# Feed-forward products whose stationary operands take every second column of a block of 256

## The chip, the cores and the metric

One core of one Trainium2 chip runs one program. The metric is the device time of that program in microseconds; the median of 3 runs of the kernel before is 1139.22 us (1137.12 to 1141.24).

## What is computed

The reference passes 256 tokens of width 1024, in float32, through seven stages with a residual stream `x`: a feed-forward (f1), a mixer of attention heads (m1), a feed-forward (f2), a second mixer (ab), a feed-forward (f3), a third mixer (cd), a feed-forward (f4), and a last norm. What matters here is the feed-forward, which has 2816 hidden columns:

```python
def _swiglu(x, w_gate, w_up, w_down):
    return (jax.nn.silu(x @ w_gate) * (x @ w_up)) @ w_down

f = _swiglu(_rmsnorm(x, ffn1_pre_g[l]), ffn1_w_gate[l], ffn1_w_up[l], ffn1_w_down[l])
x = x + 0.5 * _rmsnorm(f, ffn1_post_g[l])
```

## The kernel before

Every large product is made of three matmuls on float32r operands: each operand is split into a high part (a cast) and a low part (what the cast lost), and `mm3` (L502) adds high x high, high x low and low x high into the same accumulator in PSUM. Every matmul instruction of TensorE is two records in the trace: a weight load (LDWEIGHTS, engine PEld) that puts 128 stationary columns into the array, and a MATMUL that streams the moving operand, 256 or 512 columns wide. All these matmuls stand at L510.

Weights come as 512 KB tiles through `Stream` (L49): SyncE issues the DMA into `wraw`, ScalarE casts it to `wh` (L87), VectorE (GpSimd for a few) subtracts to `wl` (L92). There are four `wraw` buffers and six of `wh` and `wl`; a tile is split again as soon as TensorE has given its buffer back.

A feed-forward stage is `ffn` (L584). The hidden columns go in 11 blocks of 256. The first block (`first`, L599) keeps the tokens stationary and streams 256 weight columns, so its result is turned by four transposes, `ft`, at j == 1 (L631). For blocks 1 to 10, `gemm_b` (L512) makes gate and up with the weights stationary and the 256 tokens of `xh` or `xl` moving:

```python
c = slice(j * P, (j + 1) * P)
prods.append(((wh[:, k % 4, c], wl[:, k % 4, c]), (act[0][:, k, :], act[1][:, k, :])))
```

`j` is the half of the block, `k` one of 8 slices of the width, so one call is 2 x 8 x 3 = 48 matmuls into the PSUM tile `gb`, and gate and up of a block are 96. ScalarE takes silu of the gate (L636), VectorE multiplies by up (L637), and `split` (L614) writes `hh` and `hl`, 2 chunks of 128 hidden columns x 256 tokens. One block later, `down` (L566) uses a half of the tokens (128 of the 256 in `hh` or `hl`) as the stationary operand and streams 512 columns of the down weights: 2 chunks x 2 halves x 2 column halves x 3 = 24 matmuls into the tiles `f`. The last call takes four chunks (48 matmuls); in f4 some of those go to tiles `f1c`.

The order of the work is the order of the code (the scheduling is manual). `gemm_b` also serves the mixers ab and cd. Two tables at the top set where some operands start in SBUF, in bytes: `XT_AT` (L29) shifts `xh` and `xl` at each stage, by (16, 32) in f1, (64, 128) in f2, (8, 4) in f3 and (128, 224) in f4; `HH_AT` (L30) shifts `hh` and `hl` by 32, 64, 96 and 160 in f1 to f4. The tiles `wh` and `wl` stay at one place.

Other lines that the prediction names: the transposes `E` (L1310) and the plain float32 products `M` (L1317) run between blocks of f3, `za` and `zx` (L993) in ab; a product of plain float32 operands is two loads and two MATMULs in the trace, where float32r has one of each. L1027 (VectorE) and L969 (ScalarE) write or read with steps of 128 bytes, L1372 and L831 are like them with neighbouring floats.

Of the kernel before, what the change touches and what calls it, by code (L numbers as in the profile page):

```python
# [8 lines left out]
F32 = mybir.dt.float32  # L9
# [3 lines left out]
ALU = mybir.AluOpType  # L13
AX = mybir.AxisListType
P = 128
S = 256
# [170 lines left out]
class Kern:  # L187
# [321 lines left out]
                mid()  # L509
            self.nc.tensor.matmul(out=out, lhsT=l, rhs=r, start=start and i == 0, stop=stop and i == n - 1)  # L510

    def gemm_b(self, K=8, act=None):  # L512

        act = act or (self.xh, self.xl)
        tiles = self.ws.take(K // 4)
        p = self.ps("gb")
        pv = p.rearrange("p (j t) -> p j t", j=2)
        for j in range(2):
            prods = []
            for k in range(K):  # L520
                wh, wl = tiles[k // 4]
                c = slice(j * P, (j + 1) * P)
                prods.append(((wh[:, k % 4, c], wl[:, k % 4, c]), (act[0][:, k, :], act[1][:, k, :])))
            self.mm3(pv[:, j, :], prods, True, True)
            self.pump(1)
        return pv
# [39 lines left out]
    def down(self, accs, chunk, n, act, cut=False):  # L566


        tiles = self.ws.take(n)
        last = chunk + n == 22  # L570
        b2 = [(0, slice(0, 512)), (1, slice(512, D))]
        for h in range(2):
            t = slice(h * P, (h + 1) * P)
            m = n - 2 if last else n
            cs = [b2[0], (2, slice(512, 768)), (3, slice(768, D))] if last and len(accs[h]) > 2 else b2
            for i, (b, c) in [(i, b) for i in range(m) for b in cs] + [(i, b) for b in cs for i in range(m, n)]:
                ah, al = act(chunk + i)
                wh, wl = tiles[i]
                k = chunk + i
                self.mm3(accs[h][b], [((ah[:, t], al[:, t]), (wh[:, 0, c], wl[:, 0, c]))],  # L580
                         k == 0 or b > 1 and i == 0, k == 21 or cut and b == h == 1 and k == 17)


    def ffn(self, gpre, gpost, coef, gnext, hooks=None, cut=False):  # L584
        nc = self.nc
        tt = nc.vector.tensor_tensor
        with self.tc.tile_pool(name="ffn", bufs=3) as fp:
            self.php = fp
            self.nff = getattr(self, "nff", -1) + 1
            fp.tile([P, HH_AT[self.nff] // 4], F32, name="gap", tag="gap", bufs=1)  # L590
            hts = {}
            st = {}
            accs = None

            def act(c):
                hh, hl = hts[c // 2]
                return hh[:, c % 2, :], hl[:, c % 2, :]

            def first(h, mid):  # L599
                if h == 0:  # L600
                    st["w"] = self.ws.take(4)
                p = self.ps(f"fh{h}")
                t = slice(h * P, (h + 1) * P)
                for i in range(2):
                    w = st["w"][2 * i:2 * i + 2]
                    prods = [((self.xh[:, k, t], self.xl[:, k, t]), (w[k // 4][0][:, k % 4, :], w[k // 4][1][:, k % 4, :]))
                             for k in range(8)]
                    self.mm3(p[:, i * S:(i + 1) * S], prods, True, True, True, mid if i else None)
                sg = fp.tile([P, S], F32, name="sgf", tag="sgf", bufs=2)
                nc.scalar.activation(out=sg, in_=p[:, 0:S], func=AF.Silu)  # L610
                tt(out=sg, in0=sg, in1=p[:, S:2 * S], op=ALU.mult)
                st[h] = sg

            def split(t, j):  # L614
                hh = fp.tile([P, 2, S], F32R, name="hh", tag="hh")
                hl = fp.tile([P, 2, S], F32R, name="hl", tag="hl")
                nc.scalar.copy(out=hh, in_=t)  # L617
                tt(out=hl, in0=t, in1=hh.bitcast(F32), op=ALU.subtract)  # L618
                hts[j] = (hh, hl)

            self.enter(gpre, first)
            self.gain(gnext)
            if gpost:
                self.gain(gpost)
            for j in range(1, 11):
                gt = self.gemm_b()
                if j == 1:
                    p = self.ps("ft")
                    for c in range(2):
                        for h in range(2):  # L630
                            nc.tensor.transpose(p[:, c * S + h * P:c * S + (h + 1) * P], st[h][:, c * P:(c + 1) * P],  # L631
                                                self.ident)
                    split(p.rearrange("p (c t) -> p c t", c=2), 0)
                up = self.gemm_b()
                sg = fp.tile([P, 2, S], F32, name="sg", tag="sg", bufs=2)
                nc.scalar.activation(out=sg, in_=gt, func=AF.Silu)  # L636
                tt(out=sg, in0=sg, in1=up, op=ALU.mult)  # L637
                split(sg, j)
                for f in (hooks or {}).get(j, []):
                    f()  # L640
                if accs is None:
                    accs = [self.ps2("f0"), self.ps2("f1")]
                if j < 10:
                    self.down(accs, 2 * (j - 1), 2, act, cut)
            if cut:
                accs[1] += [self.ps("f1c")[:, 0:S] for _ in range(2)]
            self.down(accs, 18, 4, act)
            self.close(accs, gpost, coef)
# [978 lines left out]
def _order():  # L1627

    import numpy as np
    p = np.arange(P)  # L1630
    tau = 4 * (p % 32) + p // 32
    return np.concatenate([tau, P + tau])


def _layout(inputs):

    import numpy as np
    g = {k: np.asarray(v) for k, v in inputs.items()}
    A = {n: g[n] for n in _RAW}
    for n in ("ffn1_w_gate", "ffn1_w_up", "ffn1_w_down", "w_qkv", "w_out", "ffn2_w_gate", "ffn2_w_up", "ffn2_w_down", "x",  # L1640
              "ab_w_in_2", "ab_gate_a_w_2", "ab_gate_x_w_2", "ab_w_out_2", "cd_w_in_2", "cd_glu_w_2", "cd_w_out_2"):
        A[n] = A[n][0]
    rows = []
    for n in GAINS:
        if n.startswith("ffn_norm"):
            rows.append(g["ffn_norm_2"][int(n[-1])])
        else:
            rows.append(g[n].reshape(D))
    A["gains"] = np.stack(rows)
    A["x"] = A["x"][_order()]  # L1650
    sw = lambda a: np.ascontiguousarray(a.reshape(2, 2, 16)[:, ::-1]).reshape(64)
    q, k = g["q_norm_g"][0], g["k_norm_g"][0]
    A["gqk"] = np.stack([q, sw(q), k, sw(k)])
    ch = lambda a: a.reshape(4, P).T
    st = lambda a: a.reshape(16, 2, 64).transpose(1, 2, 0).reshape(P, 16)
    parts = {
        "convw": g["ab_conv_w_2"][0].reshape(4, 4, P).transpose(2, 0, 1).reshape(P, 16),
        "convb": ch(g["ab_conv_b_2"][0]), "ba": ch(g["ab_gate_a_b_2"][0]), "bx": ch(g["ab_gate_x_b_2"][0]),
        "lam": ch(g["ab_lambda_2"][0]), "glub": ch(g["cd_glu_b_2"][0]),
        "lr": st(g["cd_lam_re_2"][0]), "li": st(g["cd_lam_im_2"][0]),  # L1660
        "ldt": st(np.repeat(g["cd_log_dt_2"][0][:, None], 64, 1)),
        "d": np.tile(g["cd_d_2"][0].reshape(16, 32).T, (4, 1)),
    }
    A["smalls"] = np.concatenate([parts[n] for n in SM], 1)
    gb = lambda a: a.reshape(16, 2, 64, 16).transpose(1, 2, 0, 3).reshape(P, 16, 16)
    A["s5b"] = np.stack([gb(g["cd_b_re_2"][0]), gb(g["cd_b_im_2"][0])], 1)
    A["s5c"] = np.stack([gb(g["cd_c_re_2"][0].transpose(0, 2, 1)), gb(g["cd_c_im_2"][0].transpose(0, 2, 1))], 1)
    A.update(_constants())
    return {n: np.ascontiguousarray(a) for n, a in A.items()}
# [20 lines left out]
```

## Time and profile before

| | |
|---|---|
| median of 3 runs | 1139.22 us (1137.12 to 1141.24) |
| the profiled execution | 1139.47 us, its span 1137.7 us |
| granted TensorE clock, mean over the span | 0.989 |
| TensorE matmuls | 1108.9 us busy, 7435 records |
| weight loads | 1003.8 us busy |
| VectorE, ScalarE, GpSimd | 681.6, 547.0, 350.7 us busy |
| data moved | 190.99 MB, mean 168 GB/s |

The span runs from the first to the last instruction of the program. Matmuls are pipelined, and the recorded length of one (280 ns for 256 columns) is longer than the distance to the next; so the pace is read from blocks: time of a block by the number of its matmuls. The chain is the sequence of work that ended last, followed back from the end.

### The profile page before, as it was taken

What the parts mean: (1) busy time and instruction counts of PE and PEld (TensorE: products, weight loads), DVE (VectorE), ACT (ScalarE), POOL (GpSimd) and SP (SyncE); (2) the same over time, 40 slices, a digit from 0 to 9 for tenths busy, and PEclk for the clock granted to TensorE, in tenths of its full rate; (3) what the DMA queues carried; (4) which work ended last, traced back from release to release, by engine and by line L of the source; (5) the groups of instructions that cost most, each with busy time, mean ns of one, the idle gap of its engine ahead of it and who ended that gap; (6) DMA issues with size and microseconds to landing.
All of it is one profiled execution on the core that took longest, in us unless ns stands there. A gap on an engine that the chain in (4) does not pass through costs nothing.

```text
span 1137.7 us, 18727 instructions
## 1 busy us (share of the span) xinstructions
PE 1108.9 (97%) x7435; PEld 1003.8 (88%) x7435; DVE 681.6 (60%) x828; ACT 547.0 (48%) x794; POOL 350.7 (31%) x572
## 2 busy tenths in 40 slices
PE   9999999989999999999989999999999999999997
PEld 7999998767879999997966999999989889999996
DVE  5565545789575554557572666556567656554554
ACT  5456445546555443445664544444352465443442
POOL 1006600764320000004151499999414221000000
PEclk9999999999999999999988999999999999999999
DMA  7765665642057656555621675564644336657651
GB/s 233 253 198 169 189 208 163 208 166 75 20 166 235 186 161 216 185 168 173 211 81 38 185 223 174 160 204 147 191 151 149 130 101 202 204 163 220 183 169 57
DMA packets 134361, 190.99 MB, mean 168 GB/s; under 512 B 6017, under 2 KB 109441, under 8 KB 134274
## 3 DMA queue, kind: packets, MB, share of 16 engines
q1 hardware_dynamic: 133536, 187.72, 52.9%
q0 software_dynamic: 736, 2.08, 0.6%
q8 instruction: 58, 0.95, 0.3%
q14 instruction: 29, 0.24, 0.1%
q10 hardware_dynamic: 2, 0.00, 0.0%
HBM read 188.73 MB, written 1.05 MB: 167 GB/s over the span
## 4 chain that ended last, share of the span: by engine, by line
PE 86%; DVE 5%; POOL 3%; issue 2%; ACT 1%; DMA 1%; SPq 0%; POOLq 0%; DVEq 0%; ACTq 0%
PE gb L510 45%; PE f L510 20%; PE wo L510 4%; PE fh L510 4%; PE gh L510 2%; PE ga L510 1%; PE o L826 1%; PE lg L510 1%; DVE x L393 1%; PE lt L1057 1%; PE pT L806 1%; PE M L1317 1%; PE y L1394 1%; DMA wraw<-in_ffn_w_gate_dram 1%; PE tp L357 1%
## 5 line engine op out<-in xcount | busy, mean ns | idle before, releaser
L92 DVE TENSOR_TENSOR wl<-wraw,wh 128x1024 fp32r<-128x1024 f32 x323 | 398.8, 1258 | 179.6 <-ACT wh L87 177.9
L87 ACT CAST wh<-wraw 128x1024 fp32r<-128x1024 f32 x341 | 349.1, 1049 | 214.2 <-PE gb L510 116.3
L510 PE MATMUL gb<-xh,wl 128*128 128x256 f32 x1472 | 412.7, 280 | 0.0
L510 PE MATMUL gb<-xl,wh 128*128 128x256 f32 x1472 | 412.0, 280 | 0.0
L510 PE MATMUL gb<-xh,wh 128*128 128x256 f32 x1472 | 411.9, 280 | 0.0
L510 PEld LDWEIGHTS gb<-xh,wh 128*128 128x128 f32 x1472 | 277.5, 189 | 1.8
L510 PEld LDWEIGHTS gb<-xl,wh 128*128 128x128 f32 x1472 | 277.3, 188 | 1.7
L510 PEld LDWEIGHTS gb<-xh,wl 128*128 128x128 f32 x1472 | 275.8, 187 | 0.0
L510 PE MATMUL f<-wh,hh 128*128 128x512 f32 x348 | 137.3, 395 | 0.0
L510 PE MATMUL f<-wh,hl 128*128 128x512 f32 x348 | 137.0, 394 | 0.0
L510 PE MATMUL f<-wl,hh 128*128 128x512 f32 x348 | 136.9, 393 | 0.0
L617 ACT CAST hh<-sg 128x512 fp32r<-128x512 f32 x40 | 24.8, 621 | 177.5 <-DVE sg L637 177.5
L637 DVE TENSOR_TENSOR sg<-sg,gb 128x512 f32<-128x512 f32 x40 | 27.5, 687 | 119.9 <-PE gb L510 119.2
L337 POOL TENSOR_TENSOR v<-ss 128x1 f32<-128x1 f32 x22 | 5.9, 269 | 253.8 <-ACT xs L329 185.5
L92 POOL TENSOR_TENSOR wl<-wraw,wh 128x1024 fp32r<-128x1024 f32 x21 | 57.2, 2731 | 85.1 <-ACT wh L87 82.3
L332 POOL TENSOR_SCALAR ss<-ss 128x1 f32<-128x1 f32 x6 | 1.6, 270 | 252.6 <-ACT xs L329 252.6
L510 PEld LDWEIGHTS f<-wh,hl 128*128 128x128 f32 x348 | 65.4, 188 | 15.2
L510 PEld LDWEIGHTS f<-wh,hh 128*128 128x128 f32 x348 | 65.4, 188 | 13.4
L510 PEld LDWEIGHTS f<-wl,hh 128*128 128x128 f32 x348 | 65.4, 188 | 13.3
L618 DVE TENSOR_TENSOR hl<-sg,hh 128x512 fp32r<-128x512 f32 x40 | 28.2, 704 | 27.5 <-ACT hh L617 27.5
L510 PE MATMUL wo<-wl,xh 128*128 128x512 f32 x80 | 31.5, 394 | 1.0 <-POOL wl L92 1.0
L510 PE MATMUL wo<-wh,xh 128*128 128x512 f32 x80 | 32.2, 403 | 0.0
(408 smaller groups left out, 1507.7 us busy)
## 6 DMA issues: line engine op xcount, KB each, us to landing
wraw<-in_ffn_w_gate_dram SPq DMA_DIRECT2D x88, 512.0 KB, 4.1
wraw<-in_ffn_w_up_dram SPq DMA_DIRECT2D x88, 512.0 KB, 5.0
wraw<-in_ffn_w_down_dram SPq DMA_DIRECT2D x88, 512.0 KB, 4.1
wraw<-in_ab_w_in_dram SPq DMA_DIRECT2D x20, 512.0 KB, 4.5
wraw<-in_w_qkv_dram SPq DMA_DIRECT2D x18, 512.0 KB, 3.9
wraw<-in_cd_w_in_dram SPq DMA_DIRECT2D x16, 512.0 KB, 4.8
wraw<-in_w_out_dram SPq DMA_DIRECT2D x8, 512.0 KB, 4.5
wraw<-in_ab_w_out_dram SPq DMA_DIRECT2D x8, 512.0 KB, 3.5
```

What stands on the lines that cost most here:

```text
L87: self.nc.scalar.copy(out=h, in_=r)
L92: eng.tensor_tensor(out=l, in0=r, in1=h.bitcast(F32), op=ALU.subtract)
L357: nc.tensor.transpose(p[:, j * P:(j + 1) * P], src[:, (b + j) * P:(b + j + 1) * P], self.ident)
L393: nc.vector.scalar_tensor_tensor(out=xv[:, c], in0=t[:, c], scalar=r, in1=xv[:, c], op0=ALU.mult, op1=ALU.add)
L510: self.nc.tensor.matmul(out=out, lhsT=l, rhs=r, start=start and i == 0, stop=stop and i == n - 1)
L617: nc.scalar.copy(out=hh, in_=t)
L618: tt(out=hl, in0=t, in1=hh.bitcast(F32), op=ALU.subtract)
L637: tt(out=sg, in0=sg, in1=up, op=ALU.mult)
L806: nc.tensor.transpose(p[:, k * S + h * P:k * S + (h + 1) * P], e[:, h, k * P:(k + 1) * P], self.ident)
L826: nc.tensor.matmul(out=o, lhsT=v, rhs=p, start=i % 2 == 0 and n == 0, stop=i % 2 == 1 and n == 5)
L1057: nc.tensor.matmul(out=p[:, 0:384], lhsT=tri[:, 0, :], rhs=s, start=True, stop=False, skip_group_check=True)
L1317: nc.tensor.matmul(out=pv[:, a, :], lhsT=l, rhs=F[:, a, 0:4, :].rearrange("p s q -> p (s q)"), start=r == 0, stop=r == 1)
```

## The change

`gemm_b` gets a switch `deal`. With it, half `j` of a block takes the columns j, j + 2, j + 4 ... of the 256, instead of 128 neighbouring ones. So that each half still holds the same hidden columns, `_layout` reorders the gate and up weights on the host: in each block of 256, column 2i + j of the new array is column 128 j + i of the old one. The four feed-forward stages call it so; the mixers do not. In the same way `down` takes every second token of `hh` and `hl`, and `split` writes them in that order (`turn`). The first block's result comes out in the dealt order, and its transposes pick every second column. The number, order and sizes of all instructions stay as they were, on every engine; what differs is the step of operands.

```diff
--- before.py
+++ after.py
@@ -509,7 +509,8 @@
                 mid()
             self.nc.tensor.matmul(out=out, lhsT=l, rhs=r, start=start and i == 0, stop=stop and i == n - 1)
 
-    def gemm_b(self, K=8, act=None):
+    def gemm_b(self, K=8, act=None, deal=False):
 
         act = act or (self.xh, self.xl)
         tiles = self.ws.take(K // 4)
@@ -519,7 +520,7 @@
             prods = []
             for k in range(K):
                 wh, wl = tiles[k // 4]
-                c = slice(j * P, (j + 1) * P)
+                c = slice(j, None, 2) if deal else slice(j * P, (j + 1) * P)
                 prods.append(((wh[:, k % 4, c], wl[:, k % 4, c]), (act[0][:, k, :], act[1][:, k, :])))
             self.mm3(pv[:, j, :], prods, True, True)
             self.pump(1)
@@ -570,7 +571,7 @@
         last = chunk + n == 22
         b2 = [(0, slice(0, 512)), (1, slice(512, D))]
         for h in range(2):
-            t = slice(h * P, (h + 1) * P)
+            t = slice(h, None, 2)
             m = n - 2 if last else n
             cs = [b2[0], (2, slice(512, 768)), (3, slice(768, D))] if last and len(accs[h]) > 2 else b2
             for i, (b, c) in [(i, b) for i in range(m) for b in cs] + [(i, b) for b in cs for i in range(m, n)]:
@@ -614,8 +615,11 @@
             def split(t, j):
                 hh = fp.tile([P, 2, S], F32R, name="hh", tag="hh")
                 hl = fp.tile([P, 2, S], F32R, name="hl", tag="hl")
-                nc.scalar.copy(out=hh, in_=t)
-                tt(out=hl, in0=t, in1=hh.bitcast(F32), op=ALU.subtract)
+                turn = lambda ap_: ap_.rearrange("p c (t h) -> p c h t", h=2)
+                t = t.rearrange("p c (h t) -> p c h t", h=2)
+                nc.scalar.copy(out=turn(hh), in_=t)
+                tt(out=turn(hl), in0=t, in1=turn(hh).bitcast(F32), op=ALU.subtract)
                 hts[j] = (hh, hl)
 
             self.enter(gpre, first)
@@ -623,15 +627,14 @@
             if gpost:
                 self.gain(gpost)
             for j in range(1, 11):
-                gt = self.gemm_b()
+                gt = self.gemm_b(deal=True)
                 if j == 1:
                     p = self.ps("ft")
                     for c in range(2):
                         for h in range(2):
-                            nc.tensor.transpose(p[:, c * S + h * P:c * S + (h + 1) * P], st[h][:, c * P:(c + 1) * P],
-                                                self.ident)
+                            nc.tensor.transpose(p[:, c * S + h * P:c * S + (h + 1) * P], st[h][:, c::2], self.ident)
                     split(p.rearrange("p (c t) -> p c t", c=2), 0)
-                up = self.gemm_b()
+                up = self.gemm_b(deal=True)
                 sg = fp.tile([P, 2, S], F32, name="sg", tag="sg", bufs=2)
                 nc.scalar.activation(out=sg, in_=gt, func=AF.Silu)
                 tt(out=sg, in0=sg, in1=up, op=ALU.mult)
@@ -1640,6 +1643,10 @@
     for n in ("ffn1_w_gate", "ffn1_w_up", "ffn1_w_down", "w_qkv", "w_out", "ffn2_w_gate", "ffn2_w_up", "ffn2_w_down", "x",
               "ab_w_in_2", "ab_gate_a_w_2", "ab_gate_x_w_2", "ab_w_out_2", "cd_w_in_2", "cd_glu_w_2", "cd_w_out_2"):
         A[n] = A[n][0]
+    deal = lambda a: a.reshape(a.shape[:-1] + (11, 2, P)).swapaxes(-1, -2).reshape(a.shape)
+    for n in ("ffn1_w_gate", "ffn1_w_up", "ffn2_w_gate", "ffn2_w_up", "ffn_w_gate_2", "ffn_w_up_2"):
+        A[n] = deal(A[n])
     rows = []
     for n in GAINS:
         if n.startswith("ffn_norm"):
```

## Rows read from the trace of the kernel before

**Rows 1.** The page, share of the span by engine, then its chain by line.
```profile
PE 1108.9 (97%) x7435; PEld 1003.8 (88%) x7435; DVE 681.6 (60%) x828; ACT 547.0 (48%) x794; POOL 350.7 (31%) x572
...
PE gb L510 45%; PE f L510 20%; PE wo L510 4%; PE fh L510 4%; PE gh L510 2%; PE ga L510 1%; PE o L826 1%; PE lg L510 1%; DVE x L393 1%; PE lt L1057 1%; PE pT L806 1%; PE M L1317 1%; PE y L1394 1%; DMA wraw<-in_ffn_w_gate_dram 1%; PE tp L357 1%
```

**Rows 2.** The chain in order of time: start us, us, what; f1, f2, f4.
```profile
42.80 11.31 PE gb L510 x96
...
54.11 5.45 PE f L510 x24
...
358.60 11.31 PE gb L510 x96
...
369.91 5.60 PE f L510 x24
...
973.23 11.31 PE gb L510 x96
...
984.54 5.57 PE f L510 x24
```

**Rows 3.** Groups by line and shape: busy us, mean ns, idle before.
```profile
L510 PE MATMUL gb<-xh,wl 128*128 128x256 f32 x1472 | 412.7, 280 | 0.0
L510 PEld LDWEIGHTS gb<-xh,wl 128*128 128x128 f32 x1472 | 275.8, 187 | 0.0
...
L510 PE MATMUL f<-wh,hh 128*128 128x512 f32 x348 | 137.3, 395 | 0.0
...
L87 ACT CAST wh<-wraw 128x1024 fp32r<-128x1024 f32 x341 | 349.1, 1049 | 214.2 <-PE gb L510 116.3 <-ACT wh L87 25.2 <-DMA wraw<-in_ffn_w_gate_dram 22.7
L618 DVE TENSOR_TENSOR hl<-sg,hh 128x512 fp32r<-128x512 f32 x40 | 28.2, 704 | 27.5 <-ACT hh L617 27.5
```

**Rows 4.** Windows: stretch, sum, busy of PE PEld DVE ACT POOL, clock, DMA, GB/s.
```profile
42.80:54.11 11.31, 11.31 (x98) 11.31 (x97) 4.71 (x4) 3.65 (x4) 0.00 (x0) 1.00 0.83 266
54.11:59.56 5.45, 5.45 (x26) 4.50 (x26) 3.46 (x15) 4.59 (x6) 0.00 (x0) 1.00 0.05 18
668.40:679.72 11.32, 11.32 (x97) 11.32 (x97) 4.95 (x4) 3.64 (x4) 10.75 (x25) 1.00 0.85 263
679.72:685.32 5.60, 5.60 (x27) 4.49 (x26) 4.21 (x5) 3.57 (x4) 5.50 (x11) 1.00 0.14 27
```

**Rows 5.** Timeline of PE in f3: products with plain f32 operands.
```profile
696.49 1.04 PE L1310 MATMUL E<-ident,bst 128*128 128x128 f32 x8
697.36 0.39 PE L1317 MATMUL M<-Fre,b 128*128 128x128 f32 x2
697.58 0.39 PE L1317 MATMUL M<-Fim,b 128*128 128x128 f32 x2
...
698.92 0.39 PE L1317 MATMUL M<-Fim,b 128*128 128x128 f32 x2
```

**Rows 6.** Timeline of PE in ab: plain f32 products of 256 columns.
```profile
560.18 0.59 PE L993 MATMUL zx<-xc,gw 128*128 128x256 f32 x2
...
562.77 0.59 PE L993 MATMUL zx<-xc,gw 128*128 128x256 f32 x2
```

**Rows 7.** Timeline of DVE, ACT, PE at the end of f1.
```profile
189.67 0.69 DVE L618 TENSOR_TENSOR hl<-sg,hh 128x512 fp32r<-128x512 f32 x1 [0.69 <-ACT hh L617]
...
189.02 0.62 ACT L617 CAST hh<-sg 128x512 fp32r<-128x512 f32 x1 [4.97 <-DVE sg L637]
...
188.03 0.40 PE L510 MATMUL f<-wh,hh 128*128 128x512 f32 x1
```

**Rows 8.** Instructions of L1027 (128-byte steps) and, by groups, of L1372, L969, L831.
```profile
L1027 DVE TENSOR_TENSOR yrg<-tl,ga x4: 586/596/2560, 583.3 to 587.8; 128x256 f32<-128x256 f32 x4
...
L1372 DVE TENSOR_TENSOR st<-st,st 128x256 f32<-128x256 f32 x4 | 1.7, 431 | 0.1
...
L969 ACT COPY xr<-gb 128x256 f32<-128x256 f32 x4 | 1.3, 377 | 1.9 <-PE gb L510 1.9
...
L831 ACT CAST xh<-o 128x256 fp32r<-128x256 f32 x4 | 1.4, 362 | 2.4 <-PE o L826 2.2
```

## Prediction

> **What bounds the kernel now.** First the page [rows 1]: TensorE is busy for 97% of the span, and the chain that ended last is 45% `gb` (gate and up products) and 20% `f` (down products). Second the chain in order of time [rows 2]: a block of two gate and up products is 96 `gb` matmuls in 11.31 us, 117.8 ns each, and the same in f1, f2 and f4; a down block is 24 `f` matmuls, 5.45 us in f1 (227.1 ns each), 5.60 in f2 (233.3), 5.57 in f4 (232.1). f3 stands in the windows [rows 4], 11.32 and 5.60. These blocks follow each other without a hole. So inside the four feed-forward stages the time is the number of matmuls times their spacing, and nothing else. Third, does anything feed TensorE late? In the windows the granted clock is 1.00, the upper of its two levels; VectorE is busy 4.7 of 11.3 us in a `gb` block and 3.5 to 4.2 in an `f` block, ScalarE 3.6 to 4.6 [rows 4]. The cast that starts the splitting of a weight tile waits mostly for `gb` itself, 116.3 of 214.2 us of ScalarE's idle time before it [rows 3], that is for a buffer that TensorE gives back. The supply waits for the products, not the other way round. The change has to move the spacing, or it moves nothing.
>
> **What the spacing is made of.** Each matmul loads its own 128 stationary columns while the one before it streams, so both operands are read from SBUF at once. How fast could each go alone? The eight transposes `E`, each with one load and 128 columns to stream, take 696.49 to 697.36, 108.8 ns each [rows 5]: left alone, one load can follow the other at that distance. The 256 columns by which `f` is longer than `gb` cost 227.1 - 117.8 = 109 ns in f1 and 115 in f2, so 256 streamed columns alone are about 109 too. Yet `gb`, with both at once, takes 117.8: a toll of some 9 ns. Two readings say that the toll comes from where the two reads stand. `f` costs 227.1 ns in f1 and 232 to 233 in the others [rows 2, 4], and in the code those products differ only in the places of `hh` and `hl`, shifted by `HH_AT`. And `gb` costs 117.8 in all four stages, though `XT_AT` puts `xh` and `xl` at four different places. I read it so: while the load walks 512 bytes (128 neighbouring floats), the moving operand walks 1024 bytes; the faster walk overtakes the slower one, always about as often, wherever they start, and pays at each overtaking.
>
> Is there a case of equal walks? Products of plain f32 operands: each stands twice in the trace, and 256 columns of `zx` and `za` take 560.18 to 562.77 for 12 records, 215.8 ns each [rows 6], so their moving operand goes at about half of `gb`'s pace, which is the load's pace. `M` streams 128 such columns beside one load, and from 697.58 to 698.92 its 12 records take 111.7 ns each [rows 5]: 3 ns over the load's own 108.8, where `gb` pays 9.
>
> **The change, part by part.** No instruction is added, removed or moved on any engine; operands' steps change.
>
> (a) *The load of `gb`.* In the 40 pairs of gate and up products, 4 stages x 10 x 2 x 48 = 3840 of the 4416 `gb` matmuls [rows 3], the stationary operand becomes every second float of 256, so the load walks 1024 bytes, as the moving operand does. Its price stands in no row, as no stationary operand before is stepped. Bounds: 108.8 ns per matmul (the load alone), and, if a load that reaches over twice the bytes pays the toll twice, 117.8 + 6.1 = 123.9, with the toll taken against `M`'s 111.7. I take 111.7, the row of two walks at one pace, which has the same load beside it: 3840 x (117.8 - 111.7) = 23.4 us off. All of it is on the path.
>
> (b) *The load of `f`.* The stationary half of `hh` and `hl` becomes every second token, for 3 x 348 = 1044 matmuls of 512 columns [rows 3]. Bounds: 215.8 ns (512 column times without an overtaking, by `zx`) and 6 above today's. I take f1's 227.1, the best that the same instruction shows: nothing in f1, and about 260 matmuls a stage x (6.2 + 6.2 + 5.0) ns = 4.5 us off in the others.
>
> (c) *Writing `hh` and `hl`.* The 44 casts and 44 subtractions now write, and the subtractions also read, with a step of 8 bytes. The nearest rows step by 128 bytes [rows 8]: VectorE's L1027 needs 586 to 596 ns where L1372, with neighbouring floats, has 431, so 0.33 us more at 512 elements; ScalarE's L969 needs 377, against 362 for L831. I take 0 and keep 0.4 us each as the upper end. Who waits? At the end of a stage `hl` is done at 189.67 + 0.69 = 190.36, and its reader, the 15th matmul of the down block that starts at 188.03, comes 14 x 0.227 later, at 191.2 [rows 7]; `hh` (189.02 + 0.62) has over a microsecond. So 0.8 us covers it; with f's spacing at 215.8 the cover shrinks to 0.7 and still holds. In the other blocks the reader is a whole `gb` block away.
>
> (d) *The rest.* The weights are laid out on the host, and their DMAs keep shape and number. The first chunk's products stream the dealt columns side by side as before; its 16 transposes `ft` take stepped operands, and at the 6 ns of (a) that is 0.1 us either way. If TensorE goes 5% faster, the cover in the windows above (VectorE under half busy in a `gb` block) is far from used.
>
> Sum: 23.4 + 4.5 = 27.9 us off. The profiled execution took 1139.47 us (span 1137.7), 0.25 us above the median of the runs, 1139.22: so **1111.6 us**. A measurement of this kernel tells 0.3%, 3.4 us, from no change.
>
> **Rivals.**
> *Both tolls vanish.* If equal walks cost nothing, `gb` goes to 108.8 and `f` to 215.8: 3840 x 9.0 + about 260 x (11.3 + 17.5 + 17.5 + 16.3) ns = 34.6 + 16.3 = 50.9, so 1088.6. It is the lower end of the forecast, not a case apart.
>
> *A stage in step at a bad place.* Equal walks that begin in the same place stay together. If one of four stages meets that and pays twice while three gain, it is 0.75 x 27.9 - (960 + 260) x 6.1 ns = 13.5 off, 1126. Against it: `M`'s spacing shows no such lock. I count it within the forecast.
>
> *Nothing happens, 0.14.* If the excess of `gb` belongs to the moving read alone, the place of the load is without effect: 1139.5. For it: `gb` is 117.8 at all four places. Against it: `f`'s 227.1 and 233.3 at different places of the loaded operand only. The Trainium skill, "TensorE: Matmul & The Clock Gate", section "Step-by-step: what each phase is for", has this as a rule: "Loading the next tile's weights doesn't steal SBUF read bandwidth from the running matmul." By it the sum would be 0; the 6 ns between the stages' `f` speak against it.
>
> *Slower, 0.26.* The load is stretched, so it touches twice as many stretches of memory in the time of one matmul. If each costs, the toll grows with the bytes walked and not with the difference of the walks: 3840 x 6.1 + 1044 x 6.2 ns = 23.4 + 6.5 = 29.9 more, 1169. For it: the toll is paid only where the moving read is at full pace; at half pace (`M`, `zx`) it is small, which a shortage of read slots would explain as well as equal walks, and the stepped load asks for more of them. It decides when a stepped load costs more than it saves, that is above 117.8 ns in `gb`. At the far end, a load at half its pace would be 2 x 108.8 = 217.6 per `gb`, +383 us; the moving read, which fetches 1024 bytes within 117.8 ns, makes that improbable (0.02, in this case's share). The Trainium skill, "SBUF — State Buffer", section "Specifications (TRN2)", asks for at least two hits per 16-byte line for full bandwidth; a step of 8 bytes gives just two, so by it the load would keep its pace. No run so far shows a stepped load.
>
> **The numbers.** Forecast 0.60, nothing 0.14, slower 0.26. Faster 0.60, same 0.14, slower 0.26. The range begins at 1090, near the lower end of the forecast (1088.6), and reaches through no change to 1160, where the load pays some two thirds of the second toll; outside lie about 0.16 above and 0.03 below. The forecast's own range is 1090 to 1130.
>
> **What would show it.** Right: blocks of 96 `gb` in 10.7 us (111.7 each) in all four stages, `f` blocks at 5.45 or less, DMA and VectorE rows as before, `gb` in the ab and cd stages still near 117. The overtaking reading is wrong if `gb` stays at 11.3, and wrong in sign if it goes to 11.9; if it differs by stage, the starting places matter, and the stages tell the lock. (c) is wrong if TensorE sits idle before the 13th to 15th `f` matmul of a last down block. If the spacing falls and the time does not, holes between the blocks would show a late weight tile.

## The result and the profile after

The changed kernel is slower. Its median is 1147.48 us (9 runs, 1144.16 to 1152.26); 9 runs of the kernel before on the same chip have 1137.12 (1136.30 to 1141.24). The ratio is 1.0082 with a 95% interval of [1.0061, 1.0103], so some 9.3 us more by the means (6.9 to 11.7; the medians lie 10.4 apart) where the forecast had 27.9 us less.

The page of the changed kernel, the lines that answer to [rows 1]:

```profile
PE 1120.6 (97%) x7435; PEld 1023.6 (89%) x7435; DVE 684.2 (59%) x828; ACT 548.0 (48%) x794; POOL 350.6 (30%) x572
...
PE gb L510 45%; PE f L510 20%; PE fh L510 4%; PE wo L510 4%; PE ga L510 2%; PE gh L510 2%; PE o L829 1%; PE lg L510 1%; DVE x L393 1%; PE lt L1060 1%; PE y L1397 1%; DMA wraw<-in_ffn_w_up_dram 1%; PE pT L809 1%; PE M L1320 1%; PE sE L1366 1
```

The same engine is the bound, at the same share, with the same number of records; TensorE is busy 11.7 us longer and the weight loads 19.8 us. The chain in order of time (start us, us, what) shows where. The first two blocks are from f1, then two each from f2, f3 and f4; one `gb` block from the cd stage, whose loads the change left alone, stands between f3 and f4:

```profile
44.47 11.42 PE gb L510 x96
55.88 5.59 PE f L510 x24
...
363.95 11.52 PE gb L510 x96
375.47 5.58 PE f L510 x24
...
667.83 5.53 PE f L510 x24
673.35 11.64 PE gb L510 x96
...
857.50 11.31 PE gb L510 x96
...
979.00 5.56 PE f L510 x24
...
1035.70 11.49 PE gb L510 x96
```

Against [rows 2, 4] a block of 96 `gb` is longer by 0.11, 0.21, 0.32 and 0.18 us in f1 to f4: 119.0, 120.0, 121.2 and 119.7 ns per matmul, where all four had 117.8. Ten such blocks in each stage make 8.2 us. The `f` blocks changed by +0.14, -0.02, -0.07 and -0.01 us, together +0.4 us over some eleven per stage. That is 8.6 us of the 9.3, in the changed instructions alone; cd's block is unchanged. The windows of f3 say that the other engines do in them what they did before (stretch, sum, busy of PE, PEld, DVE, ACT, POOL, clock, DMA, GB/s; compare the last two of [rows 4]):

```profile
673.35:684.99 11.64, 11.64 (x98) 11.64 (x97) 4.69 (x4) 3.65 (x4) 11.15 (x25) 1.00 0.80 261
684.99:690.52 5.53, 5.53 (x27) 4.67 (x26) 3.96 (x5) 3.60 (x4) 5.27 (x12) 1.00 0.12 24
```

TensorE is busy throughout, at a granted clock of 1.00, and the tiles arrive in time. The profiled execution (1152.26 us) lies 4.8 us over its median; 2.8 us of that stand outside the changed instructions: in the second group of the very first product (`fh`), which starts 1.2 us later than before, and in a stretch of `fh` in f2 that took 5.23 us at a granted clock of 0.67 where the kernel before took 3.64 at 1.00.

The groups of loads and of the split (busy us, mean ns, idle before):

```profile
L510 PEld LDWEIGHTS gb<-xl,wh 128*128 128x128 f32 x1472 | 288.5, 196 | 1.5
...
L510 PEld LDWEIGHTS f<-wh,hh 128*128 128x128 f32 x348 | 67.8, 195 | 11.4
...
L622 DVE TENSOR_TENSOR hl<-sg,hh 128x512 fp32r<-128x512 f32 x40 | 28.6, 715 | 29.0 <-ACT hh L621 29.0
L621 ACT CAST hh<-sg 128x512 fp32r<-128x512 f32 x40 | 26.3, 658 | 179.9 <-DVE sg L640 179.9
```

A recorded load of `gb` grew from 187 ns [rows 3] to 196. The subtraction went from 704 to 715 ns. The end of f1 shows whether the slower writing matters (timeline of DVE, ACT and PE, as [rows 7]):

```profile
192.82 0.65 ACT L621 CAST hh<-sg 128x512 fp32r<-128x512 f32 x1 [5.02 <-DVE sg L640]
...
193.50 0.69 DVE L622 TENSOR_TENSOR hl<-sg,hh 128x512 fp32r<-128x512 f32 x1 [0.72 <-ACT hh L621]
```

```profile
191.83 0.40 PE L510 MATMUL f<-wh,hh 128*128 128x512 f32 x1
...
195.09 0.39 PE L510 MATMUL f<-wh,hl 128*128 128x512 f32 x1
```

`hl` is done at 194.19, its reader, the 15th matmul of that block, starts at 195.09 in an unbroken row. The stepped writes hold up no matmul there.

So what became dearer is the spacing of the very matmuls whose load steps. The experiments ask why.

### The profile page after: what moved, and what is told of

Its sections match the earlier page's. It is cut to its first block, busy times and chain, and to the rows that moved or that the text cites. A ratio compares the mean times of both kernels' runs of the same rounds, so it can differ in the third digit from the quotient of the medians.

```text
span 1150.5 us, 18727 instructions
## 1 busy us (share of the span) xinstructions
PE 1120.6 (97%) x7435; PEld 1023.6 (89%) x7435; DVE 684.2 (59%) x828; ACT 548.0 (48%) x794; POOL 350.6 (30%) x572
## 4 chain that ended last, share of the span: by engine, by line
PE 87%; DVE 5%; POOL 3%; issue 2%; ACT 1%; DMA 1%; SPq 0%; POOLq 0%; DVEq 0%; ACTq 0%
PE gb L510 45%; PE f L510 20%; PE fh L510 4%; PE wo L510 4%; PE ga L510 2%; PE gh L510 2%; PE o L829 1%; PE lg L510 1%; DVE x L393 1%; PE lt L1060 1%; PE y L1397 1%; DMA wraw<-in_ffn_w_up_dram 1%; PE pT L809 1%; PE M L1320 1%; PE sE L1366 1%
## 5 line engine op out<-in xcount | busy, mean ns | idle before, releaser
L87 ACT CAST wh<-wraw 128x1024 fp32r<-128x1024 f32 x341 | 349.2, 1049 | 222.0 <-PE gb L510 118.8
L510 PE MATMUL gb<-xh,wh 128*128 128x256 f32 x1472 | 417.7, 284 | 0.0
L510 PE MATMUL gb<-xl,wh 128*128 128x256 f32 x1472 | 416.4, 283 | 0.0
L510 PEld LDWEIGHTS gb<-xl,wh 128*128 128x128 f32 x1472 | 288.5, 196 | 1.5
L510 PEld LDWEIGHTS gb<-xh,wh 128*128 128x128 f32 x1472 | 287.1, 195 | 1.6
L510 PEld LDWEIGHTS gb<-xh,wl 128*128 128x128 f32 x1472 | 288.1, 196 | 0.0
L510 PEld LDWEIGHTS f<-wh,hl 128*128 128x128 f32 x348 | 67.8, 195 | 12.8
L510 PEld LDWEIGHTS f<-wh,hh 128*128 128x128 f32 x348 | 67.8, 195 | 11.4
L510 PEld LDWEIGHTS f<-wl,hh 128*128 128x128 f32 x348 | 67.8, 195 | 11.3
```

The lines of the kernel that those rows point to most:

```text
L87: self.nc.scalar.copy(out=h, in_=r)
```

## Experiments

The readings, named A to C in the expectations: **A**, a stepped load is slower by itself; **B**, the toll arises where the load's reads and the moving reads meet, as the prediction's overtaking has it; **C**, the toll of before belongs to the moving read alone. Unless another number is given, a kernel's time is one execution. The kernel before took 1139.43 us beside tp_steps, load0, move0 and gb_step8, 1138.67 us (median of 14) beside gb_step2, f_step2, step2_move0 and step8_move0, 1141.86 us beside both0, gb_step4, places_swap and places_before, and 1138.99 us (median of 17) beside the last three. Spacings are distances between the starts of successive matmul records; the chain's blocks of 96 or 24 give them too. Only `gb` of blocks 1 to 10 in f1 to f4 is edited unless said.

**tp_steps**: transposes on the path before each stage load `xs` with a step of 1, 2, 4, 8, 2, 4, 8 floats in f1, m1, f2, ab, f3, cd, f4 (their channels come out in another order); `cols` gives 128 columns with that step.

```diff
-                nc.tensor.transpose(p[:, j * P:(j + 1) * P], src[:, (b + j) * P:(b + j + 1) * P], self.ident)
+                nc.tensor.transpose(p[:, j * P:(j + 1) * P], src[:, self.cols(b + j)], self.ident)
```

> The kernel before, with only the 112 transposes tp changed (16 at the entry of each stage): their stationary operand steps by 1, 2, 4, 8, 2, 4, 8 floats in f1, m1, f2, ab, f3, cd, f4. The channels come out permuted, so the stages compute another function. A transpose is one load beside 128 streamed columns, 108.8 ns apart before, so it shows the pace of a load almost alone. If a stepped load is slower by itself (theory A), the spacing of these groups of eight grows with the step: 111 or more at step 2, 120 or more at 4 and 8. If a load keeps its pace at any step and only the meeting with the moving read costs (theory B), it stays at 108 to 110 at all steps.

1136.78 us. The timeline of PE, steps 1, 2, 4 and 8 in turn:

```profile
16.90 1.04 PE L364 MATMUL tp<-ident,xs 128*128 128x128 f32 x8
...
634.32 1.11 PE L364 MATMUL tp<-ident,xs 128*128 128x128 f32 x8
...
833.89 1.11 PE L364 MATMUL tp<-ident,xs 128*128 128x128 f32 x8
...
939.45 1.04 PE L364 MATMUL tp<-ident,xs 128*128 128x128 f32 x8
```

From start to start it is 109 ns at step 1, 120 at step 2, 120 to 122 at step 4, but only 109 to 114 at step 8. A holds at steps 2 and 4 and misses step 8: the price does not grow with the step here.

**load0**, **move0** and **both0** take one walk away, or both: an operand reads one column again and again, so these products compute something else. load0 stills the load, move0 the moving operand:

```diff
+                one = lambda t: t[:, k % 4, j * P:j * P + 1].to_broadcast([P, P]) if deal else t[:, k % 4, c]
+                prods.append(((one(wh), one(wl)), (act[0][:, k, :], act[1][:, k, :])))
```

```diff
+                one = lambda t: t[:, k, 0:1].to_broadcast([P, S]) if deal else t[:, k, :]
+                prods.append(((wh[:, k % 4, c], wl[:, k % 4, c]), (one(act[0]), one(act[1]))))
```

> The kernel before, with the stationary operand of the 3840 gate and up products replaced by one column read 128 times (step 0); the products are therefore others. Theory B (the toll is paid where the load's reads meet the moving reads): the load hardly reads, the spacing falls from 117.8 to 109 to 112, some 22 to 34 us less. The overtaking reading of the prediction: the walks now differ by 1024 bytes instead of 512, the toll doubles, 124 ns or more. Theory C (the toll belongs to the moving read alone): 117 to 118 stays.

> The kernel before, with the moving operand of the 3840 gate and up products replaced by one column read 256 times (step 0), the load as before; the products are therefore others. Theories B and C: 109 to 112 ns, as the moving read no longer walks. The overtaking reading: the walks still differ by 512 bytes, about 118 ns stay. If the toll is no matter of reading at all, 118 stays in this run and in the one with the load at step 0.

> Gate and up loads read one column 128 times and their moving operands one column 256 times (a changed computation in those products). Neighbouring load beside a still moving operand took 111.6 ns, a still load beside the walking one 117.7. If the load's own pace makes the 111.6, gb falls below it, to 107 to 110 ns, about 1105 us; rival 'the matmul itself takes 111.6, whatever is read': gb 111.6, about 1117 us.

load0, 1135.51 us; a block of f1, then of f2:

```profile
43.91 11.30 PE gb L510 x96
...
359.37 11.21 PE gb L510 x96
```

move0, 1116.98 us, and both0, 1113.58 us; a block of f1 each (f2 to f4 have the same):

```profile
41.74 10.72 PE gb L510 x96
```

```profile
41.21 10.72 PE gb L510 x96
```

Without the load's walk `gb` stays at 116.7 (f2) to 117.8; without the moving operand's walk it falls to 111.6, and stilling the load as well changes nothing more. So 111.6 is what the pair of instructions takes with neither operand walking, a load of neighbouring columns hides under it, and the 6 ns above it come with the moving walk; the load's own walk adds 1.1 ns in f2 and 0.2 or less in the other stages. B as the prediction had it, two walks overtaking each other, falls: it had 124 or more for load0 and 118 for move0.

**gb_step8**, **gb_step4**, **gb_step2**: the load takes every 8th, 4th or 2nd column, with weights reordered to match; nothing else. The code for step `s`, written out:

```diff
+                    o = 128 * s * (k % 4 // (s // 2)) + 2 * (k % 4 % (s // 2)) + j
+                    c = slice(o, o + s * (P - 1) + 1, s)
+                    sh, sl = (t.rearrange("p a b -> p (a b)")[:, c] for t in (wh, wl))
```

> The kernel before, with the stationary operand of the gate and up products of blocks 1 to 10 stepping by 8 floats (32 bytes), from weights laid out for it on the host; nothing else differs. Theory B, toll by the number of 16-byte pieces that a load touches (32 with neighbouring columns, 64 at step 2, 128 from step 4 on): 120 at step 2 becomes about 125 here, 1160 to 1170 us. The overtaking reading: the walks differ by 3072 bytes, six times as much as before, 140 ns or more. Theory A: what the transposes at step 8 show for a load alone, if that is above 117.

> Gate and up loads step by 4 (16 bytes), everything else as before. The load alone takes 117.7 at step 2 and 237 at step 8. If each step doubles nothing until the step leaves some line of memory (transposes at step 4: 120 to 122): gb 119 to 123 ns, about 1145 to 1155 us. Rival 'the price grows with the step': 150 to 180 ns, 1260 to 1380 us.

> Only the gate and up loads of blocks 1 to 10 step by 2, hh and hl and the first block as before. If the change's loss lies in these loads: gb 119 to 121 ns in all four stages, 3840 x 2.1 ns = 8 us over before, about 1145.5 us beside 1137.1, f at 227 in f1 and 232 to 233 in the others. Rival 'the down products carry part of it': under 4 us over before.

gb_step8, 1605.88 us, and gb_step4, 1581.67 us; a `gb` block of f1 each:

```profile
54.85 23.02 PE gb L510 x96
```

```profile
55.46 22.49 PE gb L510 x96
```

240 and 234 ns: twice the spacing of before, and far from the transposes' 110 to 122. Neither A's number nor B's had that, nor did either expectation for gb_step4; the overtaking's "140 or more" takes it in, but falls by load0 and move0. gb_step2, 5 runs, 1146.88 us, ratio 1.0063 [1.0043, 1.0082]; blocks of f1, f2 and f4:

```profile
44.02 11.42 PE gb L510 x96
...
360.93 11.52 PE gb L510 x96
...
1029.16 11.49 PE gb L510 x96
```

The loads of gate and up alone give the changed kernel's blocks back to 0.02 us, and 0.63% of its 0.82%. Whether the down products carry the rest is asked by the next kernel.

**f_step2**: the other half, only `t = slice(h, None, 2)` in `down` and the reordered writes in `split`.

> Only the down products' loads step by 2 (hh and hl written in that order), gate and up as before. If a load is hidden by the longer stream of 512 columns: f 227 in f1 and 232 to 233 elsewhere, or 230 to 233 in all as in the changed kernel, within 2 us of before, gb 117.8. Rival 'the down products carry part of the loss': 3 us or more over before.

10 runs, 1140.94 us, ratio 1.0021 [1.0006, 1.0036]. Blocks of f1 and f3:

```profile
39.08 5.60 PE f L510 x24
44.68 11.37 PE gb L510 x96
...
663.96 5.53 PE f L510 x24
669.48 11.40 PE gb L510 x96
```

`f` behaves as in the changed kernel, 233 in f1 and 230 in f3, and makes 0.4 us. More than half of the 2.3 us is not in `f`: the untouched `gb` blocks of f1 and f3 are 0.06 and 0.08 us longer than before, 1.4 us over twenty blocks, against the expectation (117.8). The changed kernel's `gb` blocks have nothing of that on top, as gb_step2, with the `f` of before, has the same ones; so the two halves don't simply add, and a rest of 0.2% is within the intervals. Why a `gb` block is longer behind another `f` block stays open. In f3 the excess lies in the first 3 us of a block, in f1 it is spread over the block, and `split` writes `hh` and `hl` during the `f` blocks, so it is not the writing that disturbs `gb`.

**step2_move0**, **step8_move0**: stepped load, still moving operand (move0's edit on the two kernels above; again these products compute something else).

> gate and up loads at step 2 (8 bytes) beside a moving operand that reads one column 256 times (a changed computation in those products). Theory 'slower of two paces' (a stream and a load each have a pace, and the later one ends the matmul): the load's own pace, read from the transposes at step 2, is 120 ns, so gb 119 to 121 ns, a block of 96 in 11.4 to 11.6 us, about 1145 us in all. Rival 'the stepped load costs only beside a walking moving read': gb 111 to 113 ns as in move0, about 1117 us.

> gate and up loads at step 8 (32 bytes) beside a moving operand that reads one column 256 times (a changed computation). With a walking moving operand gb took 240 ns. 'Slower of two paces' with the transposes' 110 to 114 ns as the load's pace: gb 112 to 114, about 1120 us, and then the 240 must come from the meeting of the load with the moving read. Rival 'the float32r load at step 8 takes 240 by itself, and the transposes differ in something else': gb 240, about 1606 us.

1140.30 and 1594.65 us. Blocks of f1:

```profile
43.88 11.30 PE gb L510 x96
```

```profile
54.64 22.70 PE gb L510 x96
```

Now the load's own price can be read: 117.7 ns at step 2, in all four stages alike (11.30), and 236.5 at step 8, both with no moving walk to meet. A is shown, and the doubling lies in the load; why a stepped load takes longer no run shows. The two-paces number was 120, taken from the transposes, and is 2 ns too high. All `gb` spacings in ns:

| the load reads | moving operand still | moving operand walks |
|---|---|---|
| one column | 111.6 | 116.7 to 117.8 |
| neighbouring columns | 111.6 | 117.8 (before) |
| every 2nd | 117.7 | 119.0 to 121.2 (the change) |
| every 4th | not run | 232 to 234 |
| every 8th | 236.5 | 240 |

At the places of before, the stepped load costs 6.1 ns by itself and the moving walk up to 6.2; together they should cost about 6 if the later of the two ends a matmul, and about 12 if they add. They cost 7.4 to 9.6. What remains over 117.7, 1.3 to 3.5 ns, differs by stage.

**places_swap** (on the changed kernel) and **places_before** (on the kernel before) move starting places alone; the edit of places_swap:

```diff
-XT_AT = ((16, 32), (64, 128), (64, 128), (64, 128), (192, 240), (192, 240), (8, 4), (96, 160), (96, 160), (128, 224))
-HH_AT = (32, 64, 96, 160)
+XT_AT = ((8, 4), (64, 128), (64, 128), (0, 0), (192, 240), (192, 240), (16, 32), (96, 160), (96, 160), (192, 240))
+HH_AT = (96, 256, 32, 32)
```

> The changed kernel with other starting places: xh and xl of f1 and f3 change places with each other, f2 gets (0, 0), f4 (192, 240); hh of f1 gets f3's 96 and f3 f1's 32, f2 256, f4 32. If the 1.2 to 3.5 ns by which gb lies over 117.7 come from where the two walks start against each other: gb about 121.2 in f1 and 119.0 in f3 (they swap), f about 230 in f1 and 233 in f3. Rival 'the stage makes the difference (its neighbours on other engines, its weights)': 119.0 in f1 and 121.2 in f3 as in the changed kernel.

> The kernel before with other starting places: xh and xl at (192, 240) in f1, (0, 0) in f2, (240, 192) in f3, (64, 128) in f4; hh at 32 in all four stages. If the place of hh sets f: 227 in all four stages, some 780 x 5.6 ns = 4.4 us off. gb: the ab stage takes 116.8 at (192, 240), so f1 goes to 116.8 if the place does it, and stays at 117.8 if the moving read's toll has nothing to do with places; f2 to f4 117 to 119. In all about 1133 us beside 1137.5.

places_swap, 1153.41 us; f1, f2, f3 and f4:

```profile
37.37 5.53 PE f L510 x24
42.89 11.64 PE gb L510 x96
...
363.08 11.52 PE gb L510 x96
...
669.62 5.59 PE f L510 x24
675.21 11.42 PE gb L510 x96
...
985.14 11.52 PE gb L510 x96
```

f1 and f3 have exchanged their numbers exactly, 11.42 with 11.64 and 5.59 with 5.53: the place makes the difference, not the stage. places_before, with `xh` and `xl` at (192, 240), (0, 0), (240, 192) and (64, 128) and `hh` at 32 throughout, 1137.98 us; f1, f2 and f3:

```profile
41.26 11.23 PE gb L510 x96
...
351.29 5.47 PE f L510 x24
356.76 11.51 PE gb L510 x96
...
659.38 5.50 PE f L510 x24
664.88 11.38 PE gb L510 x96
```

With `hh` at 32 `f` is at 5.47 to 5.50 in f2 and f3, where it was 5.60. And neighbouring loads depend on the place as well: 117.0 ns at (192, 240), 119.9 at (0, 0). The step's price is then a matter of the place, too: at (0, 0) stepped loads have just the same (11.52 in f2 of places_swap), so there it costs nothing, while at (192, 240), f4 of places_swap, they have 120.0, 3 ns more. Places alone don't settle a spacing, though: f_step2's `gb` has the places of before and other spacings in f1 and f3.

**best**, **change_placed**, **places_more**: is the excess a matter of badly chosen places, and is there a version faster than both? best is the kernel before with `XT_AT` (192, 240) and `HH_AT` 32 in all four stages, places_more the same with `xl` at 128, 192, 4 and 96; change_placed is the changed kernel with (16, 240) and 96.

> The kernel before (neighbouring loads) with xh and xl at (192, 240) and hh at 32 in all four feed-forward stages: two tables of places, nothing else. By the last run gb goes from 117.85 to 117.0 (3840 x 0.85 ns = 3.3 us off) and f to 227.5 in f2, f3, f4 (some 780 x 5.3 ns = 4.1 us off): 7.4 us, ratio 0.9935. Rival 'the gain was one run's accident': 0.998 to 1.000.

> The changed kernel with the best places that its runs have shown: xh at 16 (119.0 ns), xl at 240 (117.7 ns), hh at 96 (230.1 ns), in all four stages. If the place is all that is lost: gb 118.6, f 230.1; 3840 x 0.75 - 1044 x 1.4 ns = 1.4 us over before, ratio 1.001, and some 9 us over the unchanged loads at their own best places. Rival 'a place can be found where the stepped load costs nothing': gb 117.8 or less, ratio under 0.999.

> The kernel before with hh at 32 everywhere, xh at 192 in all four stages (116.1 ns as moving operand so far) and xl at 128, 192, 4, 96 in f1 to f4. If each moving operand has a price of its own place: two thirds at 116.1, the xl third 115 to 118; gb 115.7 to 116.8, f 227.5, about 1130 us. Rival 'what counts is the pair of successive places': some stage at 118 or more.

best, 6 runs, 1130.65 us beside 1138.99: ratio 0.9927 [0.9910, 0.9944], **faster than both kernels**. Blocks of f1 and f2:

```profile
35.89 5.45 PE f L510 x24
41.34 11.23 PE gb L510 x96
...
351.06 5.48 PE f L510 x24
356.54 11.22 PE gb L510 x96
```

10 blocks x (0.08 + 0.09 + 0.09 + 0.09) us of `gb` are 3.5 us, 780 x 5.4 ns of `f` 4.2, together 7.7 of the 8.3 measured. change_placed, 12 runs, 1140.38 us: 1.0018 [1.0003, 1.0033]:

```profile
38.16 5.52 PE f L510 x24
43.68 11.39 PE gb L510 x96
```

At places picked from its own runs the stepped load has 118.7 ns. That takes `gb`'s loss from 8.2 to 3.4 us, and `f`, at 230 in all stages, comes out 1.4 us under the unmoved kernel before; the 2 us left over that kernel are the difference of the two. Over best, which had its places picked too, it is 10: 6.8 in `gb`, 2.9 in `f`. places_more, 1134.62 us; f1 and f3:

```profile
43.29 11.40 PE gb L510 x96
...
664.28 11.51 PE gb L510 x96
```

Its four stages have 118.8, 117.8, 119.9 and 117.8 ns with `xh` at 192 in all of them. The rival held: from f1 to f4 the matmul that moves `xh` against `wh` is followed by the one that moves `xl` after 119.8, 117.5, 123.4 and 116.0 ns (means), though neither `xh` nor the weight tiles change their place, so it is the pair of successive places that counts, and a place can't be priced alone.

## Why the prediction was wrong

**Where the time is** held: the matmuls' spacing is all that moved, no engine that feeds TensorE came late, and the time followed the sum of the blocks.

**Step (a), the load of `gb`, failed**, in its sign. It put the 9 ns between 117.8 and 108.8 down to two walks of unequal pace, and took `M`'s 111.7 [rows 5] for the price of equal walks. both0 shows that 111.6 is what a load and a matmul of `gb` take with no walk at all, so `M`'s 111.7 was no sign of equal walks; what sets it for `M` wasn't tried. load0 and move0 show that the 6.1 ns over the floor go with the moving walk and stay when the load stands still (1.1 ns less in f2), so the load's walk had next to nothing to give back. And the stepped load, for which no row stood, has a price of its own: 117.7 alone, from 111.6 or less. In place of 3840 x -6.1 ns came 3840 x +2.1 (1.1, 2.2, 3.4 and 1.9 by stage): +8.2 us instead of -23.4. The rival "nothing happens" had the first half right (load0). The rival "slower" had the sign, named its point, 117.8, and blamed the stretched load, but had it pay where it meets the moving read, while the price is there with no moving walk to meet; its size was the full second toll, 123.9, and the runs give 119 to 121.2, as the two prices don't add in full. That the result lies in the range is luck as far as the forecast goes: the range reached up for that rival, and the forecast's own part ended at 1130.

The Trainium skill, "TensorE: Matmul & The Clock Gate", section "Step-by-step: what each phase is for", says that a load doesn't take read bandwidth from the running matmul. load0 agrees (116.7 to 117.8 with a load that stands still, 117.8 with one that walks); the stepped load doesn't: the moving walk beside a neighbouring load has 117.8, the stepped load beside a still operand 117.7, and both at once, at the same places, 119.0 to 121.2. In `f`, too, the place of the loaded `hh` moves the spacing, between 227 and 233. The Trainium skill, "SBUF — State Buffer", section "Specifications (TRN2)", asks for two hits per 16-byte line for full bandwidth; at 16 bytes and more (one hit) `gb` is indeed at half pace, 232 to 240, but two hits, step 2, are not free: 117.7 against 111.6. The transposes of tp_steps don't show the halving (109 to 122 ns at all steps).

**Its evidence.** That `f` costs 227 in f1 and 233 elsewhere [rows 2, 4] was read as a sign of overtaking. It is a matter of the place of `hh`: places_before and best, with `hh` at 32 in every stage, have 227 to 229 in each. And that `gb` is 117.8 in four stages was read as "wherever they start"; in f2 the records before already follow at 119.1 ns after an `xh` and 115.2 after an `xl` (means of 628 and 320), which only the average hides.

**Step (b), the load of `f`**, forecast f1's 227.1 for all stages, 4.5 us off. Measured: 233, 232.6, 230.1 and 231.7, +0.4 us in sum. The forecast took f1's number for what a load in step would have everywhere; it was that of a place. Against the same place before, the stepped load costs 6 ns at 32 (f1) and saves 3 at 96 (f3), and places_swap exchanges the two (233 and 230). None of the places tried gave a stepped `f` under 230, where neighbouring loads at 32 have 227.

**Step (c), the stepped writes**: 0, and right where it was read, at the end of f1. The cast took 37 ns more and the subtraction 11, under the 0.4 us kept as the end, and 0.9 us of cover were left.

**Step (d)**: the transposes `ft` went from 109 ns to between 118 and 132, near what tp_steps has at step 2, some 0.2 us in all where the forecast had 0.1. That the supply would keep up was never put to the test, as TensorE got no faster.

## What to carry over

Keep the columns of a stationary operand side by side: beside a float32r stream of 256 columns a step of 2 floats cost 1 to 3.4 ns of 118 at five of the six pairs of places that were run with both loads, and nothing at the sixth, (0, 0), where neighbouring columns were as slow; a step of 4 or 8 doubled the spacing. Before a toll is put down to the meeting of two reads, still each of them in turn; three kernels that read one column again and again told here what no row of the kernel before could. And a spacing that differs between stages with the same instructions is worth a look at starting places: two small tables of offsets gave 0.7% without touching an instruction.

## What was not expected of the hardware

- With a still load, a moving operand that walks over 256 float32r columns costs 116.7 to 117.8 ns per matmul; one that reads the same column 256 times, 111.6. What holds the walking read up stays open.
- The load's price jumps between steps of 8 and 16 bytes and hardly rises from there to 32: beside a walking moving operand 119 to 121.2, 232 to 234, 240.
- The transposes of plain float32 don't show that jump: 120 to 122 at 16 bytes, 109 to 114 at 32. Their load and stream differ from `gb`'s in type and length; which of these does it wasn't tried.
- Starting places, a few bytes to 240, move the same instructions by 3 ns in `gb` and 6 ns in `f`, with the operands' pair of places, and repeat from run to run to some 0.1 ns (11.64 and 11.42 exchanged). How a place sets the spacing stays open, and f_step2 shows that something besides the places has a part in it.
